# Output projection of the merge as seven block products in a stage of its own

## The chip, the core and the metric

The kernel runs on one core of a Trainium2 chip. The metric is the device time of one execution in microseconds (us); the time before is the median of three runs. The engines are TensorE (PE, with its weight loads PEld), VectorE (DVE), ScalarE (ACT), GpSimd (POOL) and SyncE (SP, which here only issues transfers). All work between them is ordered by semaphores, and each engine takes its own instructions in a fixed order.

## The reference

One encoder layer on 1024 tokens of width 1024, in float32: half a SwiGLU FFN (width 2816), a mixer of two branches (neighbourhood attention and a bidirectional state-space scan), a merge with an output projection, a second half FFN, a per-layer embedding and a last norm. What the change touches is the merge:

```python
u = rms_norm(h, mix_norm[i])
z = u @ w_in[i]
q, k, v, s_in, gates = jnp.split(z, splits, axis=-1)
y_attn = neighbourhood_attention(...) @ w_attn_out[i]
y_ssm = s5_branch(s_in, ...) @ w_ssm_out[i]
g_attn, g_ssm = jnp.split(jax.nn.sigmoid(gates), N_BRANCH, axis=-1)
h = h + (g_attn * y_attn + g_ssm * y_ssm) @ w_out[i]
h = h + 0.5 * swiglu(rms_norm(h, ffn2_norm[i]), ffn2_w_gate[i], ffn2_w_up[i], ffn2_w_down[i])
```

## The kernel before

Everything is kept transposed: a tile has 128 channels on its partitions and 512 tokens (one of two halves t = 0, 1) along it. A width of 1024 is 8 channel tiles m. The residual `h[m][t]` is 16 such tiles in one buffer (`hbuf`).

A product in float32 is made of three matmuls on rounded parts. `split` (L150 to L152) rounds a tile to `hi` on ACT (L151, CAST) and subtracts it on DVE to get `lo` (L152). `mm3` (L180 to L184) issues hi x hi, hi x lo and lo x hi as 128x128 times 128x512 matmuls (lines L182, L183, L184) into a PSUM bank; there are 8 banks.

The merge goes over four pairs of channel tiles, m0 = 0, 2, 4, 6 (L1515). For each tile and each half, `gates` (L1497) fetches two gate tiles from DRAM and applies the sigmoid on ACT (L1502); `branches` (L1489) computes the two branch projections into banks `br` (4 x 3 matmuls each); `gated` (L1506) multiplies the banks by the gates (L1509, DVE), adds the two (L1510) and splits the sum at once into `mh`, `ml`. The output projection of a pair is done by `down` (L260): for each of 8 output tiles and both halves it multiplies the pair's two merged tiles with two rows of blocks of w_out, in a bank `dn`, and adds the bank to the residual on DVE (L272): 64 evacuations in all. It runs one pair late, between the first branches of the next pair; only for the last pair it follows directly, with `merged` (L1475) as its hook: the hook squares the finished residual tile on ACT, adds it to the sum `acc` for the next RMS norm on DVE (L221, L224, L225) and writes the tile to DRAM (L1478).

Then FFN2. It does its products with seven block products in place of eight (Strassen's scheme in Winograd's form: the left operands are in `A7`, and `ACC7` = Z X Y X Y X X names the banks, L316 to L318). `Seven` norms the residual and prepares the left operands, `b_operand` (L422) the right ones, by differences of weight blocks on DVE (L426, L428). FFN2's first items are four plain quarters (banks `g`, `u`, the first one named 11). They need the norm of half 0: a PE matmul with ones sums `acc` over the partitions (`ms`, L241), `rstd` takes the reciprocal root on ACT (L203) and improves it on DVE (L204, L205, L206), the gain multiply is L390 and the operands' split gives `xh`, `xl`. This side work is a generator, `s7.first(wait, then, every)` (L402): `start` arms it, `tick` after each `mm3` counts it down, so it is laid between the matmuls in program order.

PE's order is the order of the code. DVE and ACT are ordered by a list scheduler that the build runs on a model of the program; `tc.high_priority` pulls an instruction ahead, `behind_` and `issue_after` hold one back. What it chose is fixed in the program. Transfers are issued by SP in the order of the code, those of `merged` by ACT. Buffers come from pools of fixed size (17 tiles of "m" and 20 of "w" in this stage); a new tile waits until the last reader of the one in its place has finished.

Of the kernel before, what the change touches and what calls it, by code (L numbers as in the profile page):

```python
# [38 lines left out]
def encoder_block(ctx, tc, I, out):  # L39
# [41 lines left out]
    def tmp(name, shape=(P, HT), dt=F32):  # L81
        return at("tmp", shape, dt, name)
# [4 lines left out]
    def bank(name):  # L87
        return ps.tile([P, HT], F32, tag="ps", name=name)
# [40 lines left out]
    def tick():  # L129
        if side["gen"] is None:  # L130
            return
        side["wait"] -= 1
        if side["wait"] <= 0:
            gen, side["gen"] = side["gen"], None
            w = next(gen, None)
            if w is not None:
                side["gen"], side["wait"] = gen, w
# [12 lines left out]
    def split(hi, lo, src, eng=V):  # L150
        A.copy(hi, src)  # L151
        return eng.tensor_tensor(lo, src, hi.bitcast(F32), ALU.subtract)  # L152
# [27 lines left out]
    def mm3(o, w, x, first, last, more=False):  # L180
        (wh, wl), (xh, xl) = w, x
        T.matmul(o, lhsT=wh, rhs=xh, start=first, stop=False, skip_group_check=more)  # L182
        T.matmul(o, lhsT=wh, rhs=xl, start=False, stop=False, skip_group_check=more)  # L183
        T.matmul(o, lhsT=wl, rhs=xh, start=False, stop=last, skip_group_check=more)  # L184
# [72 lines left out]
                res.append((hi, lo))  # L257
                yield every

    def down(h, t, ws, hid, scale, post=None, leads=(1,) * NK):  # L260

        n = len(ws)
        m0 = 0
        for lead in leads:
            os_ = [bank("dn") for _ in range(lead)]
            for i in range(n):
                for m, o in enumerate(os_, m0):
                    mm3(o, ws[i][m], hid[i, t], i == 0, i == n - 1)
                    tick()
            with tc.high_priority(offset=PRI):  # L270
                for m, o in enumerate(os_, m0):
                    V.scalar_tensor_tensor(h[m][t], o, scale, h[m][t], ALU.mult, ALU.add)  # L272
            if post is not None:
                for m in range(m0, m0 + lead):
                    post(m)
            m0 += lead

    def halves(h, gi, store=None):


# [138 lines left out]
                    self.put(name, self.h[j0 + k][1])  # L419
                    yield 1  # L420

    def b_operand(blk, i):  # L422

        b11, b12, b21, b22 = blk
        if i in (2, 3, 6):
            V.tensor_tensor(b11, (b12, b22, None, None, b21)[i - 2], b11, ALU.subtract)  # L426
        elif i == 5:
            V.tensor_tensor(b12, b22, b12, ALU.subtract)  # L428
        hi, lo = tw("wh", [P, HT]), tw("wl", [P, HT])
        mark["ins"] = split(hi, lo, (b21, b11, b11, b11, b22, b12, b11)[i]).ins  # L430
        return hi, lo

    NP2 = NF // 2
# [1038 lines left out]
    def h2_block(j, t):  # L1472
        return h2_d[:, (2 * j + t) * HT:(2 * j + t + 1) * HT]

    def merged(t):  # L1475
        def post(m):
            s7.nn[t].add(m)
            nc.scalar.dma_start(h2_block(m, t), h[m][t])  # L1478
        return post

    def load_h2(j, t):
        nc.sync.dma_start(h[j][t], h2_block(j, t))
# [20 lines left out]
            gts.append(gt)  # L1503
        return gts

    def gated(gts, i, t):  # L1506
        with tc.high_priority(offset=PRI):
            for b, gt in enumerate(gts):
                V.tensor_tensor(gt, banks.pop((i, t, b)), gt, ALU.mult)  # L1509
            V.tensor_tensor(gts[0], gts[0], gts[1], ALU.add)  # L1510
            hid[i, t] = (tmp("mh", dt=F32R), tmp("ml", dt=F32R))
            mark["ins"] = split(*hid[i, t], gts[0]).ins

    pend, banks, Wn = None, {}, W0
    for m0 in range(0, NK, 2):  # L1515
        W, Wn, last = Wn, [], m0 == NK - 2
        if m0 == 0:
            Wn = [loadh(I["was"][2 + i]) for i in range(2)]
        ws = [loadh(I["wout"][m0 + i]) for i in range(2)]
        hid = {}  # L1520
        if m0 == 0:

            branches(W, [(i, t, 0) for t in range(2) for i in range(2)])
        for t in range(2):
            for i in range(2):
                if t == 1 and 0 < m0 < NK - 2:
                    Wn.append(loadh(I["was"][m0 + 2 + i]))
                gts = gates(m0 + i, t)
                branches(W, [(i, t, b) for b in range(m0 == 0, 2)])
                gated(gts, i, t)  # L1530
                if pend is not None:
                    down(h, 0, *pend, 1.0)
                    down(h, 1, *pend, 1.0)
                    pend = None
            if last and t == 0:
                s7 = Seven(h, 2)
                ffn = Ffn(s7, I["wg2"], I["wu2"], I["wd2"], a2_d, load_h2, done, t0_done2, (8, 11))
                for n in (0, 2, 1, 3):
                    ffn.load_first(n)
                for g in range(2):  # L1540
                    ffn.prep(("C", "11", g))
            if last:
                down(h, t, ws, hid, 1.0, merged(t), (6, 2))
                if t == 0:
                    start(s7.first(8, 9, 1))
                else:
                    drain()
        pend = (ws, hid)


    W, phl, wpp = {}, {}, []
# [210 lines left out]
```

## Time and profile before

| | us |
|---|---|
| median of 3 runs | 2117.87 |
| the runs | 2118.72, 2116.14, 2117.87 |
| profiled execution, its own time | 2118.57 |
| span of the profiled execution | 2116.8 |
| first branch matmul of the merge | 1170.22 |
| first matmul of FFN2's second quarter | 1379.30 |

The granted TensorE clock over the span is 0.997 of full speed. In the page, busy time is counted by engine; a row of a timeline is start, duration, engine, line, operation, output and inputs, and in brackets the idle time before it with what ended it. Matmuls overlap, so the step between two starts, not the printed duration, is what one costs. A row of the windows gives a stretch of time, its length, and busy time with the number of instructions for PE, PEld, DVE, ACT and POOL, then granted clock, DMA share and GB/s.

### The profile page before, as it was taken

The page shows a single profiled execution, that of the slowest core. Times are in us where ns is not written, and L with a number is a line of the kernel's source. Part 1 is how long each engine was busy: PE and PEld are TensorE (multiplying, and loading weights), DVE is VectorE, ACT ScalarE, POOL GpSimd, SP SyncE. Part 2 cuts the span into 40 slices and gives each one's busy share as a digit, 9 for nine tenths or more (in the row PEclk, how much of TensorE's full clock was granted, in tenths as well). Part 3 has the DMA queues.
Part 4 walks back from the last instruction along what each step waited for, and adds up shares of the span by engine and source line. Part 5 has one row for each costly group of instructions (what it writes and reads, how often), then busy time and mean ns, then how long its engine had stood idle before and what let it go on. Part 6 is the DMA issues. An engine that isn't in the chain of part 4 may idle for free.

```text
span 2116.8 us, 28037 instructions
## 1 busy us (share of the span) xinstructions
PE 2089.2 (99%) x9708; PEld 1716.0 (81%) x9708; DVE 1416.2 (67%) x2416; ACT 978.3 (46%) x1793; POOL 387.3 (18%) x620
## 2 busy tenths in 40 slices
PE   8999999999999999999999999999999999999998
PEld 3788888888888888888888788788888888888886
DVE  7897776667967334777743666896565665785855
ACT  6434333334445344666764422553333334445544
POOL 0047555540000007888100000000000000000000
PEclk9999999999999999999999999999999999999999
DMA  3435444485543552223577631242423338533302
GB/s 132 142 117 153 128 130 131 138 282 157 183 120 106 157 179 67 82 82 96 150 200 260 209 105 52 93 155 95 129 80 120 100 100 290 171 107 95 116 24 80
DMA packets 195150, 280.98 MB, mean 133 GB/s; under 512 B 41280, under 2 KB 80320, under 8 KB 195008
## 3 DMA queue, kind: packets, MB, share of 16 engines
q1 hardware_dynamic: 180160, 258.22, 38.9%
q10 hardware_dynamic: 14848, 20.98, 2.9%
q8 instruction: 76, 1.25, 0.2%
q14 instruction: 66, 0.54, 0.1%
HBM read 196.81 MB, written 82.31 MB: 132 GB/s over the span
## 4 chain that ended last, share of the span: by engine, by line
PE 90%; DVE 5%; ACT 2%; DMA 1%; issue 1%; SPq 0%; DVEq 0%; ACTq 0%
PE dx L182 4%; PE dx L183 4%; PE dx L184 4%; PE ux L182 3%; PE gx L182 3%; PE ux L183 3%; PE ux L184 3%; PE gx L184 3%; PE gx L183 3%; PE gt L182 3%; PE gt L183 3%; PE gt L184 3%; PE dy L183 2%; PE dy L182 2%; PE dy L184 2%; PE uy L182 2%
## 5 line engine op out<-in xcount | busy, mean ns | idle before, releaser
L151 ACT CAST wh<-hbuf 128x512 fp32r<-128x512 f32 x280 | 172.9, 622 | 391.9 <-PE gx L183 81.9
L152 DVE TENSOR_TENSOR wl<-hbuf,wh 128x512 fp32r<-128x512 f32 x280 | 210.5, 754 | 124.3 <-ACT wh L151 122.0
L151 ACT CAST wh<-wblk 128x512 fp32r<-128x512 f32 x162 | 100.5, 623 | 166.9 <-PE dx L183 72.7
L152 DVE TENSOR_TENSOR wl<-wblk,wh 128x512 fp32r<-128x512 f32 x162 | 111.8, 692 | 46.6 <-ACT wh L151 41.2
L152 DVE TENSOR_TENSOR al<-araw,ah 128x512 fp32r<-128x512 f32 x154 | 106.4, 695 | 51.1 <-PE dx L183 21.1
L182 PE MATMUL dx<-ah,wh 128*128 128x512 f32 x352 | 137.9, 392 | 0.3 <-DVE hbuf L692 0.3
L1094 POOL TENSOR_TENSOR sc<-X,rho 128x128 f32<-128x128 f32 x128 | 78.1, 610 | 327.6 <-ACT X L1077 317.7
L184 PE MATMUL dx<-ah,wl 128*128 128x512 f32 x352 | 137.0, 389 | 0.0
L183 PE MATMUL dx<-al,wh 128*128 128x512 f32 x352 | 136.9, 389 | 0.0
L182 PE MATMUL gx<-xh,wh 128*128 128x512 f32 x320 | 124.9, 390 | 1.2 <-DVE c L579 1.2
L182 PE MATMUL ux<-xh,wh 128*128 128x512 f32 x320 | 125.1, 391 | 0.1
L184 PE MATMUL ux<-xh,wl 128*128 128x512 f32 x320 | 124.5, 389 | 0.0
L184 PE MATMUL gx<-xh,wl 128*128 128x512 f32 x320 | 124.5, 389 | 0.0
L183 PE MATMUL gx<-xl,wh 128*128 128x512 f32 x320 | 124.5, 389 | 0.0
L183 PE MATMUL ux<-xl,wh 128*128 128x512 f32 x320 | 124.5, 389 | 0.0
L151 ACT CAST ah<-araw 128x512 fp32r<-128x512 f32 x154 | 94.8, 619 | 45.6 <-PE dx L183 12.6
L182 PE MATMUL gt<-xh,wh 128*128 128x512 f32 x256 | 102.7, 401 | 0.0
L184 PE MATMUL gt<-xh,wl 128*128 128x512 f32 x256 | 99.8, 390 | 0.0
L183 PE MATMUL gt<-xl,wh 128*128 128x512 f32 x256 | 99.8, 390 | 0.0
L426 DVE TENSOR_TENSOR hbuf<-hbuf 128x512 f32<-128x512 f32 x120 | 91.3, 762 | 2.1
L182 PEld LDWEIGHTS dx<-ah,wh 128*128 128x128 f32 x352 | 66.1, 188 | 14.9 <-DVE hbuf L692 0.7
L183 PEld LDWEIGHTS dx<-al,wh 128*128 128x128 f32 x352 | 66.1, 188 | 13.9 <-issue 0.5
(376 smaller groups left out, 5719.8 us busy)
## 6 DMA issues: line engine op xcount, KB each, us to landing
araw<-a_d SPq DMA_DIRECT2D x154, 256.0 KB
a_d<-c SPq DMA_DIRECT2D x148, 256.0 KB
wblk<-in_wd SPq DMA_DIRECT2D x88, 256.0 KB
hbuf<-in_wg SPq DMA_DIRECT2D x40, 512.0 KB
hbuf<-in_wu SPq DMA_DIRECT2D x40, 512.0 KB
wst<-in_win SPq DMA_DIRECT2D x26, 512.0 KB
hbuf<-in_xT SPq DMA_DIRECT2D x32, 256.0 KB
h_d<-hbuf ACTq DMA_DIRECT2D x32, 256.0 KB
```

The costliest lines, as they stand in the source:

```text
L151: A.copy(hi, src)
L152: return eng.tensor_tensor(lo, src, hi.bitcast(F32), ALU.subtract)
L182: T.matmul(o, lhsT=wh, rhs=xh, start=first, stop=False, skip_group_check=more)
L183: T.matmul(o, lhsT=wh, rhs=xl, start=False, stop=False, skip_group_check=more)
L184: T.matmul(o, lhsT=wl, rhs=xh, start=False, stop=last, skip_group_check=more)
L426: V.tensor_tensor(b11, (b12, b22, None, None, b21)[i - 2], b11, ALU.subtract)
L1094: G.tensor_tensor(sc, both, rho4, ALU.mult)
```

## The change

`down` goes. The merge loop now only fills `mg[m, t]` (float32, 16 tiles) and no longer splits them. Behind the loop stands a stage of its own that computes the whole output projection with the seven block products: 1024 x 1024 weights are four quarters of 4 x 4 blocks, the contraction runs over 4 steps j, the outputs over 4 tiles q, so there are 7 x 4 steps of 4 `mm3` each. `out_prep` prepares a step four steps ahead: it splits the left operand (a merged tile or a sum of merged tiles, which `out_left` builds in place on DVE) and the right one with `b_operand`. The right operands' differences aren't made on DVE here: after a block has been split, `taken_from` negates it on ACT and GpSimd issues a transfer that adds the next block from DRAM onto it (`accum_op`), 16 of them. At the end of each of the seven blocks the four banks are added to the residual (L1548 of the changed kernel, 28 evacuations), and the tiles that are then final go through `merged`. FFN2's objects and first loads are made at step 4, its first two weight operands at step 12, and the norm of half 0 is armed at step 20 as `s7.first(4, 5, 2)`, before `s7.first(8, 9, 1)`. Line numbers shift: split stays L151 and L152, the gain multiply L390 is now L372, `taken_from` is L406 and L407, `gated` L1501 and L1502.

On PE, DVE, ACT, SP and POOL the rows before the merge and from FFN2's second quarter on are the same. Between them the order differs; here are the places of which the prediction speaks.

PE around the first statistic `ms` of FFN2's norm. Before, it stands inside the last branches (`br`), whose operands have long been made:

```order
L182 MATMUL br_12831<-bh_11542,whh_12342 128x512
L183 MATMUL br_12831<-bl_11543,whh_12342 128x512
L184 MATMUL br_12831<-bh_11542,whl_12343 128x512
L241 MATMUL ms_12844<-acc_12678,ones_68 128x512
L182 MATMUL br_12864<-bh_11505,whh_12387 128x512
L183 MATMUL br_12864<-bl_11506,whh_12387 128x512
L184 MATMUL br_12864<-bh_11505,whl_12388 128x512
```

In the changed kernel it stands in block 5 of the output stage, behind the first of its four steps; `dx_12442` to `dx_12454` are the four X banks:

```order
L182 MATMUL dx_12454<-ah_12746,wh_12750 128x512
L183 MATMUL dx_12454<-al_12747,wh_12750 128x512
L184 MATMUL dx_12454<-ah_12746,wl_12751 128x512
L241 MATMUL ms_12866<-acc_12396,ones_68 128x512
L182 MATMUL dx_12442<-ah_12766,wh_12770 128x512
L183 MATMUL dx_12442<-al_12767,wh_12770 128x512
L184 MATMUL dx_12442<-ah_12766,wl_12771 128x512
```

The statistic moved from the branches, which it shared with two banks in turn, into the block products, which add to the same four banks in every step.

DVE at the same place. `acc_12678` before and `acc_12396` now are the sum of squares of half 0, which the statistic reads; `wl` from `wblk` is the split of a weight block of FFN2 (before, and `wl_12409` now) or of w_out (the other `wl` now); `al` from `mg` is a left operand. Before:

```order
L225 TENSOR_TENSOR acc_12678<-acc_12678,sq_12780 128x512
L225 TENSOR_TENSOR acc_12678<-acc_12678,sq_12784 128x512
L225 TENSOR_TENSOR acc_12678<-acc_12678,sq_12804 128x512
L152 TENSOR_TENSOR wl_12691<-wblk_12667,wh_12690 128x512
L225 TENSOR_TENSOR acc_12678<-acc_12678,sq_12808 128x512
L1509 TENSOR_TENSOR gt_12812<-br_12818,gt_12812 128x512
L1509 TENSOR_TENSOR gt_12815<-br_12831,gt_12815 128x512
L152 TENSOR_TENSOR wl_12695<-wblk_12669,wh_12694 128x512
L1510 TENSOR_TENSOR gt_12812<-gt_12812,gt_12815 128x512
L204 TENSOR_TENSOR rq_12846<-rs_12679 128x512
L205 SCALAR_TENSOR_TENSOR rq_12846<-ms_12844,eps_70,rq_12846 128x512
```

and now:

```order
L152 TENSOR_TENSOR wl_12928<-wblk_12086,wh_12927 128x512
L225 TENSOR_TENSOR acc_12396<-acc_12396,sq_12826 128x512
L225 TENSOR_TENSOR acc_12396<-acc_12396,sq_12834 128x512
L152 TENSOR_TENSOR al_12847<-mg_12028,ah_12846 128x512
L152 TENSOR_TENSOR wl_12409<-wblk_12385,wh_12408 128x512
L225 TENSOR_TENSOR acc_12396<-acc_12396,sq_12842 128x512
L204 TENSOR_TENSOR rq_12868<-rs_12397 128x512
L152 TENSOR_TENSOR al_12874<-mg_12076,ah_12873 128x512
L205 SCALAR_TENSOR_TENSOR rq_12868<-ms_12866,eps_70,rq_12868 128x512
```

The last sum now stands behind the split `wl_12409`, and its ACT cast is made in a buffer that PE's step before the statistic reads. Before, the last sum stood behind `wl_12691`.

DVE at the last results of half 1. Before, L272 evacuates `dn`, in turn with the gain multiply L390 and the operands `xl`:

```order
L390 SCALAR_TENSOR_TENSOR hbuf_11551<-hbuf_11551,gains_65,rs_12679 128x512
L272 SCALAR_TENSOR_TENSOR hbuf_11551<-dn_12900,hbuf_11551 128x512
L272 SCALAR_TENSOR_TENSOR hbuf_11551<-dn_12901,hbuf_11551 128x512
L272 SCALAR_TENSOR_TENSOR hbuf_11551<-dn_12902,hbuf_11551 128x512
L152 TENSOR_TENSOR xl_12932<-hbuf_11551,xh_12931 128x512
L390 SCALAR_TENSOR_TENSOR hbuf_11551<-hbuf_11551,gains_65,rs_12679 128x512
L272 SCALAR_TENSOR_TENSOR hbuf_11551<-dn_13007,hbuf_11551 128x512
L152 TENSOR_TENSOR xl_12940<-hbuf_11551,xh_12939 128x512
L390 SCALAR_TENSOR_TENSOR hbuf_11551<-hbuf_11551,gains_65,rs_12679 128x512
L272 SCALAR_TENSOR_TENSOR hbuf_11551<-dn_13008,hbuf_11551 128x512
```

In the changed kernel the evacuations L1548 of block 5's banks, for which block 6 waits, stand behind the reciprocal root (L204 to L206) and the first operands:

```order
L206 SCALAR_TENSOR_TENSOR rs_12397<-rq_12868,rs_12397 128x512
L372 SCALAR_TENSOR_TENSOR hbuf_11551<-hbuf_11551,gains_65,rs_12397 128x512 x3
L152 TENSOR_TENSOR wl_12413<-wblk_12387,wh_12412 128x512
L152 TENSOR_TENSOR xl_12906<-hbuf_11551,xh_12905 128x512
L372 SCALAR_TENSOR_TENSOR hbuf_11551<-hbuf_11551,gains_65,rs_12397 128x512
L152 TENSOR_TENSOR xl_12917<-hbuf_11551,xh_12916 128x512
L372 SCALAR_TENSOR_TENSOR hbuf_11551<-hbuf_11551,gains_65,rs_12397 128x512
L152 TENSOR_TENSOR xl_12936<-hbuf_11551,xh_12935 128x512
L372 SCALAR_TENSOR_TENSOR hbuf_11551<-hbuf_11551,gains_65,rs_12397 128x512
L1548 TENSOR_TENSOR hbuf_11551<-hbuf_11551,dx_12442 128x512
L152 TENSOR_TENSOR wl_12411<-wblk_12389,wh_12410 128x512
L1548 TENSOR_TENSOR hbuf_11551<-hbuf_11551,dx_12446 128x512
```

All four evacuations of the block now stand together behind four turns of gain multiply and operand; before, the two took turns one by one.

The diff:

```diff
@@ -256,24 +256,6 @@
                 split(hi, lo, xn)
                 res.append((hi, lo))
                 yield every
-
-    def down(h, t, ws, hid, scale, post=None, leads=(1,) * NK):
-
-        n = len(ws)
-        m0 = 0
-        for lead in leads:
-            os_ = [bank("dn") for _ in range(lead)]
-            for i in range(n):
-                for m, o in enumerate(os_, m0):
-                    mm3(o, ws[i][m], hid[i, t], i == 0, i == n - 1)
-                    tick()
-            with tc.high_priority(offset=PRI):
-                for m, o in enumerate(os_, m0):
-                    V.scalar_tensor_tensor(h[m][t], o, scale, h[m][t], ALU.mult, ALU.add)
-            if post is not None:
-                for m in range(m0, m0 + lead):
-                    post(m)
-            m0 += lead
 
     def halves(h, gi, store=None):
 
@@ -419,15 +401,25 @@
                     self.put(name, self.h[j0 + k][1])
                     yield 1
 
-    def b_operand(blk, i):
+    def taken_from(blk, i, src):
+
+        A.activation(blk[i], blk[i], AF.Copy, scale=-1.0)
+        G.dma_start(blk[i], src, accum_op=ALU.add)
+
+    def b_operand(blk, i, src=None):
+
 
         b11, b12, b21, b22 = blk
-        if i in (2, 3, 6):
+        if src is None and i in (2, 3, 6):
             V.tensor_tensor(b11, (b12, b22, None, None, b21)[i - 2], b11, ALU.subtract)
-        elif i == 5:
+        elif src is None and i == 5:
             V.tensor_tensor(b12, b22, b12, ALU.subtract)
         hi, lo = tw("wh", [P, HT]), tw("wl", [P, HT])
         mark["ins"] = split(hi, lo, (b21, b11, b11, b11, b22, b12, b11)[i]).ins
+        if src is not None and i in (1, 2, 3):
+            taken_from(blk, 0, src[(1, 3, 2)[i - 1]])
+            if i == 2:
+                taken_from(blk, 1, src[3])
         return hi, lo
 
     NP2 = NF // 2
@@ -1472,11 +1464,9 @@
     def h2_block(j, t):
         return h2_d[:, (2 * j + t) * HT:(2 * j + t + 1) * HT]
 
-    def merged(t):
-        def post(m):
-            s7.nn[t].add(m)
-            nc.scalar.dma_start(h2_block(m, t), h[m][t])
-        return post
+    def merged(m, t):
+        s7.nn[t].add(m)
+        nc.scalar.dma_start(h2_block(m, t), h[m][t])
 
     def load_h2(j, t):
         nc.sync.dma_start(h[j][t], h2_block(j, t))
@@ -1503,22 +1493,70 @@
             gts.append(gt)
         return gts
 
-    def gated(gts, i, t):
+    def gated(gts, m, i, t):
+
+        mg[m, t] = thid("mg", dt=F32)
         with tc.high_priority(offset=PRI):
             for b, gt in enumerate(gts):
                 V.tensor_tensor(gt, banks.pop((i, t, b)), gt, ALU.mult)
-            V.tensor_tensor(gts[0], gts[0], gts[1], ALU.add)
-            hid[i, t] = (tmp("mh", dt=F32R), tmp("ml", dt=F32R))
-            mark["ins"] = split(*hid[i, t], gts[0]).ins
-
-    pend, banks, Wn = None, {}, W0
+            V.tensor_tensor(mg[m, t], gts[0], gts[1], ALU.add)
+
+    def out_place(n, j):
+
+        return I["wout"][j + (n // 2) * 4][:, (n % 2) * HT:(n % 2 + 1) * HT]
+
+    def out_load(n):
+        for j in range(4):
+            blk[j][n] = at("hid", [P, HT], F32, "wblk")
+            nc.sync.dma_start(blk[j][n], out_place(n, j))
+
+    def out_left(i, j):
+
+        a, b, c, d = (mg.get((m, t)) for t in range(2) for m in (j, 4 + j))
+
+        def s1():
+            ss[j] = thid("ss", dt=F32)
+            V.tensor_tensor(ss[j], c, d, ALU.add)
+
+        def s2():
+            V.tensor_tensor(ss[j], ss[j], a, ALU.subtract)
+            V.tensor_tensor(c, a, c, ALU.subtract)
+
+        def s4():
+            V.tensor_tensor(b, b, ss[j], ALU.subtract)
+
+        return (b, a, ss.get(j), ss.get(j), b, c, d)[i], {1: s1, 2: s2, 3: s4}.get(i)
+
+    def out_prep(i, j):
+        src, then = out_left(i, j)
+        left = tmp("ah", dt=F32R), tmp("al", dt=F32R)
+        split(*left, src)
+        made[i, j] = left, b_operand(blk[j], i, [out_place(n, j) for n in range(4)])
+        if then is not None:
+            then()
+
+    def out_run(i, j):
+        a, (hi, lo) = made.pop((i, j))
+        for q in range(4):
+            if NEW7[i] and j == 0:
+                acc[ACC7[i], q] = bank("d" + ACC7[i].lower())
+            mm3(acc[ACC7[i], q], (hi[:, ksl(q)], lo[:, ksl(q)]), a, NEW7[i] and j == 0, j == 3, not NEW7[i])
+            tick()
+            if j == 3:
+                m, t = q + (4 if i in (2, 3, 4, 5) else 0), 1 if i in (2, 5, 6) else 0
+                with tc.high_priority(offset=PRI):
+                    V.tensor_tensor(h[m][t], h[m][t], acc[ACC7[i], q], ALU.add)
+                if i in (1, 4, 5, 6):
+                    merged(m, t)
+
+    banks, Wn, mg, ss, made, acc = {}, W0, {}, {}, {}, {}
+    blk = [[None] * 4 for _ in range(4)]
+    steps = [(i, j) for i in range(7) for j in range(4)]
+    LA = 4
     for m0 in range(0, NK, 2):
-        W, Wn, last = Wn, [], m0 == NK - 2
+        W, Wn = Wn, []
         if m0 == 0:
             Wn = [loadh(I["was"][2 + i]) for i in range(2)]
-        ws = [loadh(I["wout"][m0 + i]) for i in range(2)]
-        hid = {}
-        if m0 == 0:
 
             branches(W, [(i, t, 0) for t in range(2) for i in range(2)])
         for t in range(2):
@@ -1527,25 +1565,29 @@
                     Wn.append(loadh(I["was"][m0 + 2 + i]))
                 gts = gates(m0 + i, t)
                 branches(W, [(i, t, b) for b in range(m0 == 0, 2)])
-                gated(gts, i, t)
-                if pend is not None:
-                    down(h, 0, *pend, 1.0)
-                    down(h, 1, *pend, 1.0)
-                    pend = None
-            if last and t == 0:
-                s7 = Seven(h, 2)
-                ffn = Ffn(s7, I["wg2"], I["wu2"], I["wd2"], a2_d, load_h2, done, t0_done2, (8, 11))
-                for n in (0, 2, 1, 3):
-                    ffn.load_first(n)
-                for g in range(2):
-                    ffn.prep(("C", "11", g))
-            if last:
-                down(h, t, ws, hid, 1.0, merged(t), (6, 2))
-                if t == 0:
-                    start(s7.first(8, 9, 1))
-                else:
-                    drain()
-        pend = (ws, hid)
+                gated(gts, m0 + i, i, t)
+            if m0 == NK - 2 and t == 0:
+                for s_ in steps[:LA]:
+                    out_prep(*s_)
+        if m0 in (2, 4):
+            out_load(2 if m0 == 2 else 0)
+    for n in (1, 3):
+        out_load(n)
+    for n_, (i, j) in enumerate(steps):
+        if n_ == 4:
+            s7 = Seven(h, 2)
+            ffn = Ffn(s7, I["wg2"], I["wu2"], I["wd2"], a2_d, load_h2, done, t0_done2, (8, 11))
+            for n in (0, 2, 1, 3):
+                ffn.load_first(n)
+        if n_ == 12:
+            for g in range(2):
+                ffn.prep(("C", "11", g))
+        if n_ == 20:
+            start(s7.first(4, 5, 2))
+        if n_ + LA < len(steps):
+            out_prep(*steps[n_ + LA])
+        out_run(i, j)
+    drain()
 
 
     W, phl, wpp = {}, {}, []
```

## The prediction

> **What bounds the kernel now.** I read the page first. Its busy line and its chain of waits name one engine:
>
> ```profile
> PE 2089.2 (99%) x9708; PEld 1716.0 (81%) x9708; DVE 1416.2 (67%) x2416; ACT 978.3 (46%) x1793; POOL 387.3 (18%) x620
> PE 90%; DVE 5%; ACT 2%; DMA 1%; issue 1%; SPq 0%; DVEq 0%; ACTq 0%
> ```
>
> TensorE (PE) sets the end, so the time goes down only if PE has fewer rows to issue, or waits less. I next read the windows of the stage that the change rewrites, from the first branch matmul to the first matmul after the first quarter of FFN2. The columns are the window, its length, busy time and rows of PE, PEld, DVE, ACT and POOL, then the granted TensorE clock, the DMA share and GB/s.
>
> ```profile
> 1170.20:1379.30 209.10, 202.53 (x870) 164.60 (x868) 148.26 (x227) 83.94 (x135) 0.00 (x0) 0.98 0.34 112
> 1200.00:1220.00 20.00, 18.36 (x73) 14.48 (x72) 16.34 (x27) 6.09 (x11) 0.00 (x0) 0.91 0.28 88
> 1360.00:1380.00 20.00, 18.26 (x72) 14.36 (x73) 16.94 (x28) 9.95 (x15) 0.00 (x0) 0.91 0.09 23
> 1180.00:1190.00 10.00, 10.00 (x46) 8.29 (x45) 7.13 (x11) 6.21 (x10) 0.00 (x0) 1.00 1.02 366
> ```
>
> The stage takes 209.1 us. Of its 870 PE rows two are neighbours that only touch its edges and four are passes of the two `ms` statistics, which leaves 864 matmuls: 384 `br`, 384 `dn`, 96 of FFN2. What one costs is not the printed duration (pipelined, 0.39) but the step from start to start, which the PE timeline gives:
>
> ```profile
> 1170.22 0.39 PE L182 MATMUL br<-bh,wh 128*128 128x512 f32 x1
> 1170.44 0.39 PE L183 MATMUL br<-bl,wh 128*128 128x512 f32 x1
> ...
> 1331.54 0.39 PE L184 MATMUL br<-bh,whl 128*128 128x512 f32 x1
> 1331.76 1.02 PE L241 MATMUL ms<-acc,ones 128*128 128x512 f32 x2
> 1332.22 0.79 PE L182 MATMUL br<-bh,whh 128*128 128x512 f32 x1
> 1332.85 0.39 PE L183 MATMUL br<-bl,whh 128*128 128x512 f32 x1
> ...
> 1379.30 0.39 PE L182 MATMUL g<-xh,wh 128*128 128x512 f32 x1
> ```
>
> Two starts lie 0.22 to 0.23 apart; over longer runs of rows the step is 0.2267 us, which I use. A statistic takes 1332.85 - 1331.76 - 0.23 = 0.86. So the stage's work is 864 x 0.2267 + 2 x 0.86 = 197.6, and 209.1 - 197.6 = 11.5 us are lost. The same timeline shows where:
>
> ```profile
> 1208.75 0.39 PE L184 MATMUL dn<-mh,whl 128*128 128x512 f32 x1
> 1210.55 0.49 PE L182 MATMUL dn<-mh,whh 128*128 128x512 f32 x1 [1.41 <-ACT mh L151]
> 1211.27 0.61 PE L183 MATMUL dn<-ml,whh 128*128 128x512 f32 x1 [0.23 <-DVE ml L152]
> ...
> 1215.02 0.40 PE L183 MATMUL dn<-ml,whh 128*128 128x512 f32 x1
> ...
> 1351.02 0.39 PE L182 MATMUL g<-xh,wh 128*128 128x512 f32 x1
> ...
> 1355.58 0.50 PE L183 MATMUL g<-xl,wh 128*128 128x512 f32 x1 [0.90 <-DVE xl L152]
> ...
> 1361.74 2.08 PE L241 MATMUL ms<-acc,ones 128*128 128x512 f32 x2 [2.70 <-DVE acc L225]
> ...
> 1365.70 0.39 PE L182 MATMUL u<-xh,wh 128*128 128x512 f32 x1
> ```
>
> From 1208.75 to 1215.02 PE makes 11 steps, 2.5 us of work, in 6.3: 3.8 lost, 1.4 of it a wait for the split of the merged tile, and most of the rest a slower clock behind the wait (from 1211.27 to 1215.02 nine steps of 0.42, and the clock is 0.91 in that window). From 1351.02 to 1365.70 it makes 27 steps and a statistic, 7.0 us, in 14.7: 7.7 lost to DVE's operands `xl`, to DVE's sums for the second statistic, and to the clock again. 3.8 + 7.7 is the 11.5. Everywhere else in the stage PE runs warm and back to back.
>
> **Part 1: fewer matmuls.** `down` did 8 output tiles x 2 halves x 8 contraction tiles x 3 = 384 matmuls. The seven block products do 7 x 4 steps x 4 tiles x 3 = 336. PE loses 48 rows: 48 x 0.2267 = **10.9 us**. Nothing hides or cancels this, since PE issues all of its rows in order; only new waits could.
>
> **Part 2: the old waits go, 11.5 us.** The wait at 1210.55 was for the split of a merged tile which the next `dn` needed at once. Now no split stands between a gated tile and the next PE row: the branches only fill banks, DVE empties them into `mg`, and the first split is consumed after all the branches. Gate and weight transfers come earlier in SP's queue, because the loads of w_out no longer stand ahead of them, so I expect no wait in the 87.0 us of branches (384 x 0.2267). The wait at 1361.74 and those on `xl` came from FFN2's first operands and eight L272 evacuations taking turns on DVE. Those exact turns are gone too, but similar ones come in.
>
> **Part 3: new waits in the output stage.** One step is 12 matmuls, 2.72 us, one block 10.9 us, the stage 76.2. Let T be 0 at its first matmul. Operands are prepared four steps (10.9 us) ahead, and each of the banks Y (blocks 2, 4) and X (1, 3) is revisited with another block between. Four evacuations of about 0.6 us fit there, so through block 4 DVE and ACT keep slack. Two places do not. DVE's pitches and ACT's cast come from these rows:
>
> ```profile
> 1341.74 2.07 DVE L390 SCALAR_TENSOR_TENSOR hbuf<-hbuf,gains,rs 128x512 f32<-128x512 f32 x3
> 1343.73 0.69 DVE L272 SCALAR_TENSOR_TENSOR hbuf<-dn,hbuf 128x512 f32<-128x512 f32 x1
> 1344.34 0.68 DVE L152 TENSOR_TENSOR xl<-hbuf,xh 128x512 fp32r<-128x512 f32 x1
> 1344.93 0.75 DVE L390 SCALAR_TENSOR_TENSOR hbuf<-hbuf,gains,rs 128x512 f32<-128x512 f32 x1
> 1345.60 0.69 DVE L272 SCALAR_TENSOR_TENSOR hbuf<-dn,hbuf 128x512 f32<-128x512 f32 x1
> ...
> 1364.58 0.69 DVE L204 TENSOR_TENSOR rq<-rs 128x512 f32<-128x512 f32 x1 [2.89 <-ACT rs L203]
> 1365.30 0.75 DVE L205 SCALAR_TENSOR_TENSOR rq<-ms,eps,rq 128x512 f32<-128x512 f32 x1
> ```
>
> ```profile
> L151 ACT CAST wh<-wblk 128x512 fp32r<-128x512 f32 x162 | 100.5, 623 | 166.9 <-PE dx L183 72.7
> ```
>
> An ordinary DVE operation steps 0.60, the gain multiply 0.66, a link of the reciprocal-root chain about 0.72.
>
> *(a)* The first statistic stands on PE right behind step 0 of block 5 (T = 57.1). It waits for DVE's last sum into `acc`, and that stands in DVE's queue behind the split of an FFN2 weight block (`wl` from `wblk`), whose ACT cast takes a buffer that PE's last matmuls before the statistic still read. So cast 0.62, subtract 0.60, sum 0.70 follow PE's last row in series, about **2.0 us** with the hand-overs. What is queued behind: all of PE's next three steps.
>
> *(b)* Block 6 goes into the same X banks as block 5, with no block between. Its first matmul waits for the evacuation (L1548) of block 5's first tile. But block 5's evacuations stand in DVE's queue behind the whole reciprocal root and four norm-and-split pairs. From the statistic's start: 2.84 to L204 (1364.58 - 1361.74, the row above, which also came after a wait); then L204, L205, L206 at about 0.7 with three splits `al` between, 3.9; three gain multiplies 2.0; `wl` 0.6; three turns of `xl` and a gain multiply, 3.8; the evacuation 0.7. Together 13.8. PE has in that time 0.86 + 36 x 0.2267 = 9.0 of work. It loses **4.8 us**; a slower clock during these 9.0 is hidden by the wait itself.
>
> *(c)* After (b) the clock is slow again, as it was after 1.41 us at 1210.55: nine steps at 0.42 are 1.7, with the first step **1.9 us**.
>
> The Trainium skill ("TensorE: Matmul & The Clock Gate", Part 1: The HAM clock gate) has the clock halve after about 3.4 us of idling. By that the wait of 4.8 us might or might not slow the clock, and without (c) the time would be 2102.3. The row of 1210.55, slow after 1.41, speaks against so long a threshold.
>
> Then block 6 runs, its evacuations and the second sums have all of FFN2's first 96 matmuls to finish, and I expect no third wait. Sum: 2.0 + 4.8 + 1.9 = 8.7, between 2.0 (the evacuation is taken early enough) and 12 (each of the two waits cools the clock fully).
>
> **Part 4: the accumulating transfers.** 16 new transfers of 256 KB on GpSimd's queue each add a weight block onto a block that ACT has negated. GpSimd is idle here (0.00 in the stage's window), so nothing else is queued behind them. In the trace of before no transfer accumulates and none comes from that queue. Bounds: moved at the window's 366 GB/s, 256 KB take 0.72 us; the longest wait for a finished transfer of this size between two SP transfers is 5.2, in the queue's waits:
>
> ```profile
> SPq L1418 <- DMA y_d<-sg: 12.2, 4, 5.2
> ```
>
> The first four are issued during the branches. Eight more must be done between about T = 1.6 and the read at T = 40.8: they may take 39.2 / 8 = 4.9 us each, one after another, before PE waits. I take about 3, nearer to the low row because the stage's DMA share is only 0.34, so the cost is **0**. It is ACT's cast behind a late transfer, and then PE, that would pay.
>
> **Sum.** The profiled execution took 2118.57 (span 2116.8 and 1.8 around it): 2118.6 - 10.9 - 11.5 + 8.7 = 2104.9. The median of the three runs is 2117.87, so the forecast for the median is 2117.9 - 13.7 = **2104.2 us**, 0.65% faster. A measurement of this kernel can tell about 0.2%, 4.2 us, from no change.
>
> **Rivals.**
>
> *The new waits are smaller (0.15).* If (a) hides in idle time of DVE, or the clock holds, 2 to 8 of the 8.7 us vanish; at most the gain is 22.4, 2095.5, and typically 2099. For: DVE is idle for 61 of the 209 us of the stage. Against: DVE's order is fixed, and the idle is before it.
>
> *The gain is half lost (0.14).* DVE's new work (16 operand sums, 28 evacuations) or the transfers run late once more, at the second block, as in the row of 1210.55: 3.8 us, or twice that. 2108 to 2112. In the same case belongs that the stage turns out to be bound by DVE in each block, and the gain is spent: about 2116. For: DVE is 148 of 209 busy. Against: 56 splits, 28 evacuations and 16 sums over 28 steps are 3.6 operations a step, 2.1 us of 2.7.
>
> *The accumulating transfers are late (0.08), slower than before.* They are a chain: negate, add, split, negate again, for four rows each. If each of the eight takes over 4.9 us, PE waits 8 times the excess; from 4.9 + 13.7 / 8 = 6.6 us each the kernel is slower than before. At 8 us: 24.8 lost, 2129. For: the row of 5.2 is past 4.9 (5.2 would cost 2.4). Against: transfers of one queue may overlap, and 366 GB/s leaves seven times the room.
>
> The Trainium skill ("SBUF — State Buffer", the box "The DVE blocks DMA trap (SWDGE)" and "A bandwidth-pool intuition that's wrong") says that transfers issued from GpSimd starve for descriptors while VectorE runs an operation in a two-port mode, 620 ns growing to 3100. That would be this rival's mechanism; its 2.5 us more on my 3 come to 5.5 each, 4.8 us late. No run so far shows it, and DVE here runs mostly operations with two inputs.
>
> *The change does not act (0.03).* The 48 rows are gone from the program, so this could only be if waits fill exactly their place: 2115 to 2119.
>
> **How the numbers follow.** My forecast (gain 10 to 17.5, 2100.4 to 2107.9) has 0.60. The range takes in half of the first rival and most of the second: 2097.5 to 2111.5, which leaves out about 0.2. Faster by over 0.2%: 0.60 + 0.15 + 0.11 = 0.86; within 0.2%: 0.06; slower: 0.08.
>
> **What would show it.** In the profile after: no idle of PE between the first `br` and the first `dz`; 87.0 us of branches; 7 blocks of 10.9 us without gaps through block 4; a wait of about 2 us before the first `ms`, released by DVE `acc`; a wait of about 5 us at the first `dx` of block 6, released by DVE `hbuf` L1548; about ten slow steps behind it; from the first `br` to the second quarter of FFN2 195.4 us in place of 209.1. It is wrong if PE waits on ACT casts of `wblk` behind GpSimd's transfers, or on L1548 at blocks 3 and 4, or if time moves outside this stage.

## The result and the profile after

The changed kernel takes 2106.16 us (median of 6 runs, 2104.76 to 2109.11), the kernel before beside it 2117.1 (6 runs, 2115.63 to 2120.48): a ratio of 0.9948, 95% interval 0.9935 to 0.9960, or 10.9 us less, with an interval of about 8.5 to 13.8. The forecast was 13.7 less. The profiled execution took 2106.49, its span 2104.7.

The chain of waits, by engine, is now still more PE's (90% before):

```profile
PE 93%; DVE 4%; ACT 1%; DMA 1%; issue 1%; SPq 0%; DVEq 0%; ACTq 0%
```

The windows of the rewritten stage, first as a whole (209.10 before, with 870 PE rows), then cut at the first `dz`, ahead of the first statistic, and behind block 6's first steps:

```profile
1172.21:1367.05 194.84, 188.65 (x821) 154.77 (x820) 145.94 (x230) 105.29 (x174) 14.14 (x16) 0.99 0.48 142
1172.21:1259.25 87.04, 87.04 (x385) 72.07 (x384) 53.77 (x81) 44.61 (x73) 3.66 (x4) 1.00 0.69 225
1259.25:1316.00 56.75, 56.75 (x252) 47.00 (x251) 50.02 (x83) 33.27 (x60) 10.49 (x12) 1.00 0.48 94
1316.00:1336.00 20.00, 13.81 (x52) 10.36 (x51) 17.92 (x29) 12.01 (x20) 0.00 (x0) 0.91 0.17 64
1336.00:1367.05 31.05, 31.05 (x136) 25.34 (x135) 24.24 (x39) 15.40 (x23) 0.00 (x0) 1.00 0.12 45
```

Read down the PE column: the branches take 87.04 us and PE is busy for all of them; so it is through block 4 (56.75 of 56.75) and after block 6 has begun (31.05 of 31.05). All that is lost lies in the one window of 20 us where PE is busy for 13.81 and the clock is at 0.91. Its PE timeline:

```profile
1316.15 0.39 PE L184 MATMUL dx<-ah,wl 128*128 128x512 f32 x1
1319.14 1.12 PE L241 MATMUL ms<-acc,ones 128*128 128x512 f32 x2 [2.61 <-DVE acc L225]
...
1320.34 0.39 PE L183 MATMUL dx<-al,wh 128*128 128x512 f32 x1
...
1328.07 0.39 PE L184 MATMUL dx<-ah,wl 128*128 128x512 f32 x1
1332.04 0.76 PE L182 MATMUL dx<-ah,wh 128*128 128x512 f32 x1 [3.58 <-DVE hbuf L1548]
1332.60 0.63 PE L183 MATMUL dx<-al,wh 128*128 128x512 f32 x1
...
1335.10 0.39 PE L183 MATMUL dx<-al,wh 128*128 128x512 f32 x1
```

From 1316.15 to 1320.34 PE has two steps and a statistic to make, 1.31, in 4.19: 2.9 lost. From 1328.07 to 1335.10 it has eight steps, 1.81, in 7.03: 5.2 lost. 2.9 + 5.2 = 8.1, and 194.84 less 8.1 is the work: 336 + 384 + 96 = 816 matmuls at 0.2267 and two statistics are 186.7. The stage is 14.2 us shorter than before's 209.08, of which 10.9 are the rows and 3.4 the difference of what is lost, 11.5 and 8.1.

The whole is 12.1 shorter between the two profiled executions, because the stage began later: 1172.21 where it was 1170.22. That is taken up below.

### The profile page after: what moved, and what is told of

It is laid out like the page before. It is cut to its first block, busy times and chain, and to the rows that moved or that the text cites. A ratio compares the mean times of both kernels' runs of the same rounds, so it can differ in the third digit from the quotient of the medians.

```text
span 2104.7 us, 28050 instructions
## 1 busy us (share of the span) xinstructions
PE 2077.2 (99%) x9660; PEld 1707.4 (81%) x9660; DVE 1414.2 (67%) x2420; ACT 1000.3 (48%) x1832; POOL 401.7 (19%) x636
## 4 chain that ended last, share of the span: by engine, by line
PE 93%; DVE 4%; ACT 1%; DMA 1%; issue 1%; SPq 0%; DVEq 0%; ACTq 0%
PE dx L182 4%; PE dx L183 4%; PE dx L184 4%; PE ux L182 3%; PE ux L184 3%; PE ux L183 3%; PE gx L182 3%; PE gx L183 3%; PE gx L184 3%; PE gt L182 3%; PE gt L183 3%; PE gt L184 3%; PE dy L183 2%; PE dy L182 2%; PE dy L184 2%; PE uy L182 2%
## 5 line engine op out<-in xcount | busy, mean ns | idle before, releaser
L151 ACT CAST wh<-hbuf 128x512 fp32r<-128x512 f32 x280 | 172.9, 622 | 392.3 <-PE gx L183 84.0
L152 DVE TENSOR_TENSOR wl<-hbuf,wh 128x512 fp32r<-128x512 f32 x280 | 210.4, 754 | 125.2 <-ACT wh L151 123.0
L151 ACT CAST wh<-wblk 128x512 fp32r<-128x512 f32 x190 | 117.8, 622 | 182.5 <-PE dx L183 78.5
L182 PE MATMUL dx<-ah,wh 128*128 128x512 f32 x416 | 164.0, 394 | 3.9 <-DVE hbuf L1548 3.6
L152 DVE TENSOR_TENSOR wl<-wblk,wh 128x512 fp32r<-128x512 f32 x190 | 130.3, 688 | 53.4 <-ACT wh L151 48.0
L184 PE MATMUL dx<-ah,wl 128*128 128x512 f32 x416 | 162.3, 390 | 0.0
L183 PE MATMUL dx<-al,wh 128*128 128x512 f32 x416 | 162.3, 390 | 0.0
L152 DVE TENSOR_TENSOR al<-araw,ah 128x512 fp32r<-128x512 f32 x154 | 106.0, 692 | 53.7 <-PE dx L183 21.1
L151 ACT CAST ah<-araw 128x512 fp32r<-128x512 f32 x154 | 95.0, 619 | 47.5 <-PE dx L183 12.7
L182 PEld LDWEIGHTS dx<-ah,wh 128*128 128x128 f32 x416 | 78.4, 188 | 21.8 <-issue 4.7
L183 PEld LDWEIGHTS dx<-al,wh 128*128 128x128 f32 x416 | 78.5, 189 | 16.8 <-issue 0.7
```

## Experiments

Their times stand beside runs of the kernel before on the same chip. What decides is mostly the stage's length, from the first `br` to the first matmul of FFN2's second quarter, and in it what PE loses against its work of 186.7 (197.6 with 48 rows more), worked out as above, gap by gap; it can be up to 0.2 less than the stage minus that work, since the step is rounded.

| kernel | median us | ratio to before, 95% | first `br` | stage | lost |
|---|---|---|---|---|---|
| before | 2117.1 | | 1170.22 | 209.08 | 11.5 |
| before_again | 2119.15 (one run) | | 1170.70 | 209.15 | 11.5 |
| changed | 2106.16 | 0.9948 (0.9935 to 0.9960) | 1172.21 | 194.84 | 8.1 |
| after_again | 2106.58 (one run) | | 1171.31 | 195.86 | 9.1 |
| both_waits | 2099.43 | 0.9916 (0.9903 to 0.9930) | 1170.98 | 189.58 | 2.8 |
| evac_first | 2101.46 | 0.9923 (0.9911 to 0.9936) | 1170.99 | 191.28 | 4.5 |
| dve_sums | 2104.92 | 0.9944 (0.9931 to 0.9958) | 1169.01 | 196.75 | 9.9 |
| held_dve_sums | 2105.24 | 0.9938 (0.9924 to 0.9951) | 1169.34 | 194.87 | 8.0 |
| double_adds | 2107.08 | 0.9949 (0.9936 to 0.9961) | 1168.39 | 196.96 | 10.2 |
| plus_48 | 2113.91 | 0.9985 (0.9976 to 0.9994) | 1171.47 | 203.74 | 6.1 |
| before_evac_first | 2117.26 | 0.9997 (0.9988 to 1.0006) | 1172.47 | 207.03 | 9.4 |

**Are the two waits what is left?** The theory: PE's loss in the new stage is DVE's order at two places. The rival: behind each stands the next late thing, and nothing is won by mending it. *both_waits* holds the split of an FFN2 weight pair behind the last sum; by that, the scheduler also sets block 5's evacuations ahead:

```diff
-                eng.tensor_tensor(self.acc, self.acc, sq, ALU.add)
+                self.ins = eng.tensor_tensor(self.acc, self.acc, sq, ALU.add).ins
...
         if n_ == 20:
             start(s7.first(4, 5, 2))
+        if n_ == 22:
+            with tc.issue_after(s7.nn[0].ins):
+                for g in range(2):
+                    ffn.prep(("C", "12", g))
```

> The changed kernel with one addition: the splits of FFN2's second pair of weight operands (wl from wblk) are held on DVE behind the last sum for the first statistic. DVE's order then has block 5's evacuations (L1552 here) ahead of the gain multiplies. Theory 1 (the loss left in the stage is the two waits on DVE's order): the 2.61 us wait before the first ms shrinks to about 1, the 3.58 wait before block 6 to about 0.5, the slow steps behind it (1.5) go; together 6 us, about 2100 where the changed kernel has 2106. Theory 2 (PE would meet the next late thing at once, a weight split of block 6 or an operand of FFN2): the same time as the changed kernel within 2 us, with a new wait named wl, xl or ACT cast in the profile.

Its PE timeline at the same two places:

```profile
1316.48 1.12 PE L241 MATMUL ms<-acc,ones 128*128 128x512 f32 x2 [1.18 <-DVE acc L225]
1326.30 0.47 PE L182 MATMUL dx<-ah,wh 128*128 128x512 f32 x1 [0.51 <-ACT wh L151]
```

2.61 has become 1.18, 3.58 has become 0.51 (and that one for a weight cast on ACT), and the slow steps are gone. The stage is 5.3 us shorter than the changed kernel's, the time 6.7 (in the profiled executions it also began 1.2 earlier). The first theory stands; this version is the fastest of all, 17.6 us ahead of before.

*evac_first* takes only the second place, by arming the norm later:

```diff
         if n_ == 20:
-            start(s7.first(4, 5, 2))
+            start(s7.first(4, 14, 1))
```

> The changed kernel with the side work of the first norm armed as (4, 14, 1) in place of (4, 5, 2): the statistic stays where it is, the operands' norm comes 14 ticks behind it. On DVE the evacuations of block 5 then stand ahead of the turns of gain multiply and xl; the sum behind the weight split before the first ms stays. Theory 1: the wait before ms stays at 2.6 us, that before block 6 falls from 3.58 to about 0.7, and the slow steps behind it go: 4.4 us less, about 2102. Theory 2 (the norm, pushed back, is late for FFN2's first quarter): the gain is given back there, PE waits on xl or xh in g, 2106 or more.

```profile
1317.93 1.78 PE L241 MATMUL ms<-acc,ones 128*128 128x512 f32 x2 [2.62 <-DVE acc L225]
```

The wait before the first `ms` is there as before (2.62, with the clock slow behind it, 4.5 lost in all), that before block 6 is gone altogether. The time is 2101.5 where 2102 was expected. So the norm's turns ahead of the evacuations were the cause of the second wait, and FFN2's first quarter could do without them so early. That nothing at all is left of it is partly the slow clock: it cost PE 1.9 us behind the first wait, so PE came to block 6 later; with a fast clock some of the expected 0.7 could have remained.

**Do the rows count?** *plus_48* does the first block product twice.

```diff
+            if i == 0:
+                mm3(acc[ACC7[i], q], (hi[:, ksl(q)], lo[:, ksl(q)]), a, j == 0, False)
-            mm3(acc[ACC7[i], q], (hi[:, ksl(q)], lo[:, ksl(q)]), a, NEW7[i] and j == 0, j == 3, not NEW7[i])
+            mm3(acc[ACC7[i], q], (hi[:, ksl(q)], lo[:, ksl(q)]), a, NEW7[i] and j == 0 and i != 0, j == 3, not NEW7[i])
```

> The changed kernel with the first block product (bank Z) done twice in each step: 48 matmuls more, as many as before, everything else in place (the Z product is counted twice in the output). Theory 1 (each PE row costs its step, 0.2267 us): 10.9 us slower than the changed kernel, about equal to before (2117). Theory 2 (the gain comes from the layout, and the rows fill idle time somewhere): less than 5 us slower.

It takes 2113.9, 7.8 more than the changed kernel, between the two theories. The stage tells why: the scheduler orders DVE otherwise for the longer program, and the wait before block 6 is two short ones:

```profile
1329.25 1.12 PE L241 MATMUL ms<-acc,ones 128*128 128x512 f32 x2 [2.57 <-DVE acc L225]
1341.71 0.50 PE L182 MATMUL dx<-ah,wh 128*128 128x512 f32 x1 [0.19 <-DVE hbuf L1550]
1343.58 0.50 PE L182 MATMUL dx<-ah,wh 128*128 128x512 f32 x1 [0.90 <-DVE hbuf L1550]
```

It loses 6.1 where the changed kernel lost 8.1: 203.74 - 194.84 = 8.9 is 10.9 for the rows less 2.0 of waits. All 48 rows are paid in full; there was no idle time that they could fill.

**What do the accumulating transfers cost, and what do they buy?** In the changed kernel GpSimd's line, with the time from issue to landing:

```profile
L407 POOL DMA_DIRECT2D wblk<-in_wout x16: 856/864/1774, 1242.7 to 1285.2; - x16
DMA to landing us min/median/max: 4.0/6.2/9.4
```

Landing takes 6.2 us, and still PE waits for none. *double_adds* issues each twice, the second behind the first's landing (each block is added twice, so the weights' sums are other ones).

```diff
-        G.dma_start(blk[i], src, accum_op=ALU.add)
+        for _ in range(2):
+            G.dma_start(blk[i], src, accum_op=ALU.add)
```

> The changed kernel with every accumulating transfer issued twice, the second waiting for the first to land (the sums of weight blocks are then other ones: each block is added twice). Theory 1 (transfers overlap, landing takes about 6 us, and about 10.9 us lie between a negation and the next read of the block): the doubled chain of about 13 us is late by some 2 us a turn and is hidden by the four steps of lookahead, so 0 to 3 us slower. Theory 2 (they cost one after another, as my 4.9 us each had it): twice 6.2 is far over 4.9, 8 x 7.5 = 60 us slower. Theory 3: GpSimd's queue is held up by the second transfer's wait, about 5 to 20 us slower, PE waiting behind ACT casts of wblk.

Its waits, total, times and longest:

```profile
POOL wblk L408 <- DMA wblk<-in_wout: 32.4, 10, 7.3
ACT wh L151 <- DMA wblk<-in_wout: 13.3, 5, 4.3
```

GpSimd's queue stands for 32.4 us and ACT for 13.3, and the time is 2107.1, the stage 1 to 2 us longer than in two executions of the changed kernel. PE names none of it; its wait before the first `ms` is 3.73 where it was 2.61. So the lookahead hides twice the transfers but for 1 to 2 us, and theory 2's reckoning, 6.2 us each one after another, is refuted. Whether the 1.1 more before `ms` comes from the transfers or from another order on DVE is open: DVE once stood 4.3 us for a weight cast that waited for a transfer, and its order in this stretch is another one too.

*dve_sums* does the differences on DVE, without transfers.

```diff
-        made[i, j] = left, b_operand(blk[j], i, [out_place(n, j) for n in range(4)])
+        made[i, j] = left, b_operand(blk[j], i)
```

> The changed kernel with the differences of w_out's blocks made on DVE (16 subtracts) instead of ACT's negation and GpSimd's accumulating transfers. Theory 1 (the transfers are hidden, their cost is 0, and DVE has slack through block 4): the same time, 2106 within 2 us. Theory 2 (the transfers cost something, by contention or through ACT's casts behind them): faster by 1 to 5. Theory 3 (DVE has no room): 16 x 0.6 = 9.6 us of DVE work in some 45 us makes the evacuations late at blocks 3 or 4, slower by 2 to 6.

The time is 1.2 us shorter than the changed kernel's, which taken alone says "no difference". The stage says otherwise: it is 1 to 2 longer, with 3.6 lost in blocks 2 and 3, where PE now waits for `al` on DVE, and less than before at block 6, by another order. Two effects nearly cancel, and the earlier start (1169.01) hides the rest. *held_dve_sums* adds the edit of both_waits, so that only the differences remain:

> The kernel of both_waits (FFN2's second weight pair held behind the last sum) with the differences of w_out's blocks made on DVE, as in dve_sums. There the stage lost 3.6 us in blocks 2 and 3, PE waiting for al on DVE, but by another order of the scheduler less before block 6, so that the two nearly cancelled. Theory 1 (the transfers take 16 operations off DVE at a place where it has too little room): the 3.6 us stay, and no chance gain hides them: the stage takes 193.2 where both_waits has 189.6, the time about 2103 to its 2099.4. Theory 2 (DVE's slack suffices once the order at the end is another): 189.6 and 2099.4 within 1 us.

```profile
1290.41 0.50 PE L183 MATMUL dx<-al,wh 128*128 128x512 f32 x1 [1.00 <-DVE al L152]
1298.22 0.50 PE L183 MATMUL dx<-al,wh 128*128 128x512 f32 x1 [2.04 <-DVE al L152]
```

The windows around these rows, and the same stretch of both_waits behind them:

```profile
1284.00:1299.00 15.00, 11.96 (x51) 9.23 (x50) 15.00 (x26) 11.75 (x22) 0.00 (x0) 1.00 0.10 36
1286.00:1301.00 15.00, 15.00 (x68) 12.43 (x67) 13.94 (x24) 8.66 (x16) 0.00 (x0) 1.00 0.08 15
```

Against both_waits the stage is 5.3 us longer and the time 5.8 (4.7 by the ratios to before, as the two ran on different chips): 1.3 and 3.9 are lost around these two rows. That is what the transfers buy: 16 operations off DVE, which is busy for all of the 15.00 us where it has to make them and for 13.94 where it has not. It is more than theory 1 had, since the clock went slow behind the wait of 2.04; behind a wait of 2.1 at the same place in dve_sums it stayed fast, and there the two waits cost 3.6.

**Could before have had its share without the change?** *before_evac_first* arms the norm later in the kernel before, `s7.first(8, 24, 1)` for `(8, 9, 1)`.

> The kernel before, with the side work of the first norm armed as (8, 24, 1) in place of (8, 9, 1): on DVE the evacuations L272 of half 1 then stand together, ahead of most turns of gain multiply and xl. Theory 1 (the 7.7 us lost at the end of the stage before were DVE's load: from 1341 to 1361 it has no idle time, in whatever order): the loss stays within 2 us, 2115 to 2118. Theory 2 (it was the order alone, as in the changed kernel at block 6): the 7.7 go, about 2109, and then most of the second half of the gain of the change could have been had without it.

Its waits of PE for `xl` in the stage (before had 2.2 in 3, and the 2.70 before the second `ms`, which is gone here):

```profile
PE g L183 <- DVE xl L152: 3.7, 5, 1.5
```

The windows over 20 us of the end of the stage, in the kernel before and then in this one, which began 2.25 us later:

```profile
1341.00:1361.00 20.00, 15.81 (x66) 11.79 (x65) 19.66 (x32) 13.11 (x20) 0.00 (x0) 1.00 0.28 105
1343.25:1363.25 20.00, 16.25 (x67) 11.60 (x65) 19.76 (x32) 10.22 (x18) 0.00 (x0) 1.00 0.28 105
```

The order changed, the loss at the end of the stage went from 7.7 to 5.5, a little more than theory 1 allowed, and the time is the same within its interval (0.9997, 0.9988 to 1.0006). So 2.2 us of the 7.7 were the order. DVE has next to no idle time there in either order, which speaks for its load as the cause of the other 5.5; that no order would have saved them isn't shown. Nor was it tried whether the 3.8 us lost at 1210.55 could have been had without the change.

**The later start.** The rows ahead of the merge are the same in both kernels, and yet the stage began 2.0 us later.

> The kernel before once more, for its profile. The question is whether the first branch matmul of the merge starts at 1170.2 in each execution; in the changed kernel it started at 1172.2. If the 2.0 us are of one execution (PE waits of the scan stage and the clock behind them), the start varies by 1 to 3 us here too, and by as much between the runs of the other kernels. If they belong to the changed kernel, this is 1170.2 within 0.3.

> The changed kernel once more, for its profile. If the 2.0 us ahead of the merge belong to one execution, the first branch matmul starts between 1170 and 1173; if they belong to the changed kernel, at 1172.2 within 0.3. The stage itself should take 194.9 within 1 us, with waits of about 2.6 before the first ms and 3.6 before block 6.

The starts are 1170.70 and 1171.31; over all eleven executions they lie between 1168.39 and 1172.47, and those of the kernel before and its variant (1170.22, 1170.70, 1172.47) lie among those of the changed kernel and its variants. So the 2.0 us are within what executions differ by; their cause wasn't looked for. After_again also shows that the loss in the stage is not the same each time. Here the clock went slow behind the first wait, and the second came out shorter:

```profile
1318.24 1.90 PE L241 MATMUL ms<-acc,ones 128*128 128x512 f32 x2 [2.61 <-DVE acc L225]
1319.15 1.41 PE L182 MATMUL dx<-ah,wh 128*128 128x512 f32 x1
1320.37 0.63 PE L183 MATMUL dx<-al,wh 128*128 128x512 f32 x1
...
1331.91 0.58 PE L182 MATMUL dx<-ah,wh 128*128 128x512 f32 x1 [2.71 <-DVE hbuf L1548]
```

## Why the prediction was right, point by point

The time (2106.16 to 2104.2 forecast) is right in sign and place, and in mechanism but for two points, the series in (a) and the price of the transfers; the stage, for which 195.4 stood on record, took 194.84 and 195.86.

*Part 1, fewer matmuls, 10.9.* Right, and shown by plus_48: put back, they cost 10.9 within the stage.

*Part 2, the old waits go.* Right: no PE wait from the first `br` through block 4. Before_evac_first adds that of the 7.7 lost at the end only 2.2 went with another order. The rest looks like DVE's load: in the changed kernel DVE is busy for 24.24 of the last 31.05 us, where before it had 19.66 of 20.00. That this is why the loss went is argued, not tested.

*Part 3, new waits.* Both came where they were foretold, released as foretold. (a) was put at 2.0 and was 2.61 in both executions. The working let the cast, the subtract and the sum follow PE's last row in series. The timelines of ACT and DVE after show another cause:

```profile
1310.95 0.62 ACT L151 CAST wh<-wblk 128x512 fp32r<-128x512 f32 x1 [2.14 <-PE dy L183]
...
1315.86 0.60 ACT L151 CAST ah<-mg 128x512 fp32r<-128x512 f32 x1
1316.40 0.62 ACT L151 CAST wh<-wblk 128x512 fp32r<-128x512 f32 x1
```

```profile
1311.61 0.69 DVE L152 TENSOR_TENSOR wl<-wblk,wh 128x512 fp32r<-128x512 f32 x1 [2.07 <-ACT wh L151]
1312.21 1.88 DVE L1548 TENSOR_TENSOR hbuf<-hbuf,dy 128x512 f32<-128x512 f32 x3
1314.01 0.68 DVE L225 TENSOR_TENSOR acc<-acc,sq 128x512 f32<-128x512 f32 x1
1314.61 0.68 DVE L1548 TENSOR_TENSOR hbuf<-hbuf,dy 128x512 f32<-128x512 f32 x1
1315.21 0.68 DVE L152 TENSOR_TENSOR wl<-wblk,wh 128x512 fp32r<-128x512 f32 x1
1315.81 1.48 DVE L225 TENSOR_TENSOR acc<-acc,sq 128x512 f32<-128x512 f32 x2
1317.21 0.68 DVE L152 TENSOR_TENSOR al<-mg,ah 128x512 fp32r<-128x512 f32 x1
1317.81 0.68 DVE L152 TENSOR_TENSOR wl<-wblk,wh 128x512 fp32r<-128x512 f32 x1
1318.41 0.68 DVE L225 TENSOR_TENSOR acc<-acc,sq 128x512 f32<-128x512 f32 x1
```

The last cast began as soon as ACT had ended the one before and was over at 1317.02, but DVE took its split `wl` up only at 1317.81. From 1311.61 to the last sum DVE makes 11 operations in 6.8 us, 0.60 each but for 0.2. So its full queue, with three splits `wl` in it, set the wait, and not the buffer that PE's last rows held; that 2.0 came near was luck in part. The split that did wait for PE is the first of the three: its cast stood 2.14 us for a row of block 4. In both_waits the last sum has no `wl` shortly ahead of it:

```profile
1315.14 0.69 DVE L152 TENSOR_TENSOR al<-mg,ah 128x512 fp32r<-128x512 f32 x1
1315.74 0.68 DVE L225 TENSOR_TENSOR acc<-acc,sq 128x512 f32<-128x512 f32 x1
1316.35 1.89 DVE L152 TENSOR_TENSOR wl<-wblk,wh 128x512 fp32r<-128x512 f32 x3
```

(b) was put at 4.8 and was 3.58 and 2.71. The term that was mis-sized is the way from the statistic to L204, taken as 2.84 from a row that followed a slow clock. DVE in the changed kernel, and last the row of after_again:

```profile
1321.03 0.69 DVE L204 TENSOR_TENSOR rq<-rs 128x512 f32<-128x512 f32 x1 [1.94 <-ACT rs L203]
...
1330.55 0.74 DVE L372 SCALAR_TENSOR_TENSOR hbuf<-hbuf,gains,rs 128x512 f32<-128x512 f32 x1
1331.21 0.68 DVE L1548 TENSOR_TENSOR hbuf<-hbuf,dx 128x512 f32<-128x512 f32 x1
...
1320.90 0.69 DVE L204 TENSOR_TENSOR rq<-rs 128x512 f32<-128x512 f32 x1 [2.71 <-ACT rs L203]
```

From 1319.14 to 1321.03 are 1.89, with the clock fast. In after_again, with the clock slow, 1318.24 to 1320.90 are 2.66, near the 2.84; there PE's own rows took longer too, and so its wait came out shorter. From L204 to the evacuation 10.2, where the working had 10.3. (c), 1.9 for the clock, was 1.6 (5.22 less 3.58). In the sum the errors offset: 8.7 forecast, 8.1 and 9.1 measured.

*Part 4, the accumulating transfers, 0.* The result was right, no PE wait names them, and its reason was not: I took about 3 us each, one after another, against a threshold of 4.9. They land 6.2 us after issue (median), over the threshold, but this is the time from issue to landing of one among several in flight. Five were issued in a row from 1263.40 on and landed after 5.8 to 8.5 us. In the window 1263 to 1276 their queue (q0) kept the 16 DMA engines busy throughout:

```profile
DMA packets 1178, 2.17 MB, mean 167 GB/s; under 512 B 128, under 2 KB 128, under 8 KB 1177
q0 software_dynamic: 1177, 2.15, 102.2%
```

At 167 GB/s 256 KB take 1.6 us, an estimate from this row. So one after another they cost about 1.6 each, far under 4.9, and by the program at least four steps, 10.9 us, lie between a negation and the next read of its block, which is more than the landing takes. Double_adds fits this: two landings in series go past 10.9, and then ACT and GpSimd wait. The rival on this point needed over 6.6 us for each in turn.

The 2.8 us between the forecast and the measured gain are not in the stage, and the interval of the gain, 8.5 to 13.8, just takes in the 13.7. Across the eleven profiles the start of the merge scatters by 4 us, so a difference of this size in the whole time can't be given to a cause.

## What to carry to other kernels

Where the bounding engine stands without a gap, as here, removed rows are worth rows times step; the uncertainty is in the queues of the engines that feed it, and much of these can be read ahead from the order and the durations. Look there for two things: a sum that the bounding engine needs, queued behind splits that it needs later, and an evacuation queued behind work that is needed later than the bank is. Add up the whole queue from its last idle time on, not only the link nearest to the wait. Judge an experiment by the stage, not by the whole time alone: dve_sums hid a loss of 3.6 us in two blocks behind a chance gain of order and an earlier start.

## What the runs showed of the hardware

Waits of the same length did not always leave the clock the same: 2.61 us before the first `ms` left it fast in one execution of the changed kernel (next steps 0.23) and slow in another (0.43 for some four steps), 1.41 left it slow in before, and 1.18 fast in both_waits. Where it was slow, the steps were about 0.43, nearly twice 0.2267, and 1.6 to 2.1 us were lost beside the wait. The Trainium skill ("TensorE: Matmul & The Clock Gate", Part 1: The HAM clock gate) speaks of a free-running window of about 3.4 us that halves the clock; the step of 0.43 and the dependence on chance agree with that, but that an idle time of 1.41 sufficed does not agree with a whole idle window, and here the measured rows decide.

Accumulating transfers of 256 KB from GpSimd landed 4.0 to 9.4 us after their issue (median 6.2), and GpSimd issued one in 0.86 (median). 12 of the 16 fell in the window in which DVE was busy for 50.02 of 56.75 us; the last four, issued one at a time from 1273.34 on, landed after 4.0 to 4.2, five issued in a row after 5.8 to 8.5.
